# Moving two SBUF tiles by 96 bytes: `region` and `xs` at 448 instead of 32 modulo 512

## The chip, the cores and the metric

The kernel runs on one core of one Trainium2 chip. The metric is the device time of one execution in microseconds (us); the time before is the median of three runs. A profile is a hardware trace of one execution. Its engines are PE (TensorE matmul), PEld (TensorE weight load), DVE (VectorE), ACT (ScalarE), POOL (GpSimd) and SP (SyncE, which issues the DMAs). SBUF is the memory on the chip that the engines read: 128 partitions, and in each of them a tile takes a stretch of bytes. An address below is a byte offset within a partition, given modulo 512.

## The reference, cut to what matters

Two encoder layers over 256 positions of width 1024, in float32. Each layer is half a gated feed-forward block, a mixer, and another half block:

```python
for l in range(DEPTH):
    x = x + 0.5 * swiglu(rmsnorm(x, ffn1_norm[l]), ffn1_w_gu[l], ffn1_w_down[l])
    ...
    x = x + mix
    x = x + 0.5 * swiglu(rmsnorm(x, ffn2_norm[l]), ffn2_w_gu[l], ffn2_w_down[l])
```

`swiglu(h, w_gu, w_down)` splits `h @ w_gu` in two halves of 2816 columns, `g` and `u`, and returns `(silu(g) * u) @ w_down`. The mixer of layer 0 is a chunked spatial gate beside differential attention, that of layer 1 latent attention beside grouped attention with rotary embedding; both have one projection in and one out. The feed-forward products are the bulk of the work.

## The kernel before, in words

**Precision.** A float32 product is made from two parts of each operand. `hi` is the value rounded to the matmul type (`F32R`), `lo` what is left. A product is then hi x hi + lo x hi + hi x lo, three full-rate passes, of which the feed-forward blocks do a part only.

**Weights.** SP's queue loads pieces of 1 MB into four `raw` tiles. For each half of a piece ACT copies it to a `hi` tile and DVE subtracts to get a `lo` tile (`fetch`, line 481); there are six of each. They are used in the order of the program.

**Activations.** `x` stays in SBUF, transposed: model dimension on the partitions, positions along the row. `xs` (line 570) holds its scaled `hi` and `lo` parts, for each of 8 k-tiles 2 x 256 elements, so 2048 bytes a k-tile. `region` is an arena of 11264 elements, which each stage cuts anew: the feed-forward blocks put `hs`, the 22 tiles of hidden activations, in it (2048 bytes each), the mixers their projections and `os_`, the operand of the output product.

**Matmul loops.** A matmul has a stationary operand, which PE loads as weights (128 columns, 512 bytes), and a moving one, which it streams.

- `wide` (line 552), feed-forward: stationary is a 128 x 128 chunk of `hi`, moving is `flat(x2)`, 512 columns, the hi and lo part of one k-tile of `xs` or `hs`; then stationary is the same chunk of `lo`, moving the first 256 of these columns. One such pair for each chunk.
- `dense` (line 544): three matmuls, (xh, wh), (xh, wl), (xl, wh). In `out_product` (line 642) the weights are stationary and 256 columns of `os_` in `region` are moving. In `block` (line 616), the input projections, it is the other way round: stationary are 128 columns of `xs`, and a row of `hi` or `lo` of width `w` is moving: 512 columns mostly, 256 in the odd layer's `k` block and 416 in its `c` block (line 623 has the offset, `k % per * w`).

**The order.** All operations are recorded in a `Program` (line 82), with a cost and a priority each. `schedule` (line 162) lists them by a model of the engines and of free slots, and `emit` (line 274) issues them in that order. What depends on what is found from tile names and the offsets inside a tile (`touched`, line 93); the place of a tile in SBUF plays no part.

**Placement.** `keep(name, ...)` (line 373) makes one tile that lives throughout. Tiles lie one behind another in the order in which they are made, each rounded up to a multiple of 32 bytes, and the first, `t1_0`, starts at 128. `scratch` tiles `t1` (1024 bytes) and `t2` (2048) come first; then 32 small tiles `sm` of 20 elements (96 bytes each with the rounding), which `Turns` hands out in rotation, one after another (line 376); then `gap0`, 128 bytes that nobody uses; `raw`, `hi`, `lo`; `region32`, 21888 bytes; `gx` (with `x`), 8448 bytes; `ident`, `ones`, `onesr`, 512 bytes each; `warm`, one element; `gap1`, unused; `region`, `xs`; and behind them `rr`, `rb`, `acc`, `acc2`, rotary tables and small values.

`warm` (line 450) takes the result of one activation at the start, which makes ACT load a function table early. No operation reads it.

Of the kernel before, what the change touches and what calls it, by code (L numbers as in the profile page):

```python
# [351 lines left out]
def trunk_kernel(ctx: ExitStack, tc: tile.TileContext, a: dict, out: bass.AP):  # L352
# [20 lines left out]
    def keep(nm, *shape, dt=F32):  # L373
        return sb.tile([P, *shape], dt, name=nm)
# [38 lines left out]
    sm = Turns("sm", 32, 20)  # L413
# [33 lines left out]
    nc.vector.memset(ones, 1.0)  # L447
    onesr = keep("onesr", P, dt=F32R)
    nc.vector.tensor_copy(out=onesr, in_=ones)
    warm = keep("warm", 1)  # L450
    nc.scalar.activation(out=warm, in_=ones[:, :1], func=AF.Silu)
    make_identity(nc, ident)
    with lead(90e3):
# [112 lines left out]

    keep("gap1", 32)
    region, xs = keep("region", ARENA, dt=F32R), keep("xs", KT, 2, N, dt=F32R)  # L570
    rr_, rb, acc, acc2 = keep("rr", 2), keep("rb", N), keep("acc", N), keep("acc2", 2, N, dt=F32R)
    rr = [rr_[:, h:h + 1] for h in range(2)]
# [589 lines left out]
```

## Time and profile before

| | |
|---|---|
| time, median of 3 runs | 941.68 us (941.42 to 942.18) |
| the profiled execution | 941.91 us |
| its span, first to last instruction | 940.1 us |
| granted TensorE clock | 0.999 |
| PE busy | 933.7 us, 5564 matmuls |
| DVE busy | 723.9 us |
| ACT busy | 548.3 us |
| DMA, whole span | 167.83 MB, mean 179 GB/s |

The difference between the profiled execution and its span is what lies before the first and behind the last recorded instruction. Matmuls are pipelined: the duration of one runs until its results are out, and the next one starts before that, so the sum of durations is more than the busy time, and the cost of a matmul in a steady loop is the distance from its start to the next start. Nearly every operation has line 285 of the kernel, since `emit` issues it there; groups are told apart by the names of their tiles, `out<-in`, with buffer numbers left out: `bank<-xs,hi` is a matmul into a PSUM bank with `xs` moving and a `hi` tile as weights, or `bank<-hi,xs` the reverse.

### The profile page before, as it was taken

The numbers are of one execution on the slowest core, as the hardware profiler recorded it, in microseconds if no ns is written. First come the engines' busy times: TensorE is split into PE (matmuls) and PEld (weight loads), VectorE is DVE, ScalarE is ACT, GpSimd is POOL, SyncE is SP. The second block draws the span as 40 slices with busy tenths as digits, with TensorE's granted clock in tenths as the row PEclk, the third lists the DMA queues.
The fourth block names the chain that finished last, engine by engine and source line by source line (L and its number), as shares of the span: only waits on it lengthen the run. The fifth ranks groups of instructions, "written<-read, shape, count | busy, mean of one in ns | idle before, by whom it ended". The sixth has DMA issues, their size and how long they took to land.

```text
span 940.1 us, 14528 instructions
## 1 busy us (share of the span) xinstructions
PE 933.7 (99%) x5564; PEld 829.3 (88%) x5564; DVE 723.9 (77%) x1326; ACT 548.3 (58%) x938; POOL 27.5 (3%) x57
## 2 busy tenths in 40 slices
PE   9999999999999999999999999999999999999998
PEld 8888888888899888888888888888989988888887
DVE  7997776579989878876588887756888698878652
ACT  7765655446956656655465666544587566565530
POOL 0910000000000000000000000000000000000000
PEclk9999999999999999999999999999999999999999
DMA  9775555553255555555555555554412355555530
GB/s 337 258 268 180 182 192 204 184 180 135 97 217 174 185 190 204 188 180 186 204 181 192 183 195 205 180 184 163 179 57 86 106 186 201 180 185 201 200 109 22
DMA packets 26421, 167.83 MB, mean 179 GB/s; under 512 B 2928, under 2 KB 5104, under 8 KB 7024
## 3 DMA queue, kind: packets, MB, share of 16 engines
q1 hardware_dynamic: 26352, 166.92, 50.4%
q8 instruction: 43, 0.70, 0.3%
q14 instruction: 26, 0.21, 0.1%
HBM read 165.86 MB, written 1.05 MB: 178 GB/s over the span
## 4 chain that ended last, share of the span: by engine, by line
PE 97%; DVE 1%; ACT 1%; DMA 0%; issue 0%; SPq 0%; ACTq 0%
PE bank L285 97%; DVE t L285 0%; ACT t L285 0%; DMA raw<-in_gu 0%; DVE sm L285 0%; ACT hi L285 0%; DVE region L285 0%; DVE lo L285 0%; ACT L285 0%; DVE hi L285 0%; DVE ssg L285 0%; DVE gx L285 0%; SPq L285 0%; DVE ssc L285 0%; DVE rc L285 0%
## 5 line engine op out<-in xcount | busy, mean ns | idle before, releaser
L285 DVE TENSOR_TENSOR lo<-raw,hi 128x1024 fp32r<-128x1024 f32 (+2 forms) x318 | 382.2, 1203 | 161.6 <-ACT hi L285 155.9
L285 ACT ACTIVATE hi<-raw 128x1024 fp32r<-128x1024 f32 (+3 forms) x310 | 322.7, 1043 | 299.7 <-PE bank L285 188.3
L285 PE MATMUL bank<-xs,hi 128*128 128x512 f32 x1408 | 490.8, 391 | 0.5 <-ACT hi L285 0.5
L285 PE MATMUL bank<-xs,lo 128*128 128x256 f32 x1408 | 398.2, 283 | 0.0
L285 PEld LDWEIGHTS bank<-xs,hi 128*128 128x128 f32 x1408 | 265.4, 188 | 56.2 <-ACT hi L285 0.8
L285 PE MATMUL bank<-region,hi 128*128 128x512 f32 (+1 forms) x982 | 290.8, 357 | 0.0
L285 PEld LDWEIGHTS bank<-xs,lo 128*128 128x128 f32 x1408 | 267.2, 190 | 0.7 <-DVE lo L285 0.7
L285 PE MATMUL bank<-region,lo 128*128 128x256 f32 x832 | 234.2, 282 | 0.0
L285 PEld LDWEIGHTS bank<-region,hi 128*128 128x128 f32 x982 | 173.8, 188 | 27.0
L285 PEld LDWEIGHTS bank<-region,lo 128*128 128x128 f32 x832 | 157.1, 189 | 0.0
L285 ACT ACTIVATE t<-bank 128x256 f32<-128x256 f32 (+1 forms) x201 | 76.8, 401 | 40.5 <-PE bank L285 39.4
L285 PE MATMUL bank<-hi,xs 128*128 128x512 f32 (+2 forms) x256 | 78.5, 381 | 0.0
L285 DVE TENSOR_TENSOR t<-bank,t 128x256 f32<-128x256 f32 x176 | 67.5, 420 | 1.0 <-ACT t L285 1.0
L285 DVE TENSOR_TENSOR t<-t,rb 128x512 f32<-128x512 f32 x88 | 60.3, 688 | 1.2
L285 PEld LDWEIGHTS bank<-hi,xs 128*128 128x128 f32 x256 | 47.1, 188 | 8.5
L285 DVE SCALAR_TENSOR_TENSOR gx<-bank,gx 128x256 f32<-128x256 f32 (+1 forms) x71 | 28.3, 450 | 27.2 <-PE bank L285 27.2
L285 PE MATMUL bank<-lo,xs 128*128 128x512 f32 (+2 forms) x128 | 48.1, 375 | 0.0
L285 DVE TENSOR_TENSOR t<-t,t 128x256 f32<-128x256 f32 (+2 forms) x108 | 45.8, 428 | 0.1
L285 ACT ACTIVATE t<-t 128x256 f32<-128x256 f32 (+2 forms) x98 | 39.1, 406 | 3.1 <-DVE t L285 3.1
L285 DVE TENSOR_TENSOR region<-t,region 128x256 fp32r<-128x256 f32 (+2 forms) x92 | 39.1, 429 | 1.1 <-ACT region L285 1.1
L285 ACT ACTIVATE region<-t 128x256 fp32r<-128x256 f32 (+1 forms) x89 | 35.6, 405 | 1.5 <-DVE t L285 1.2
L285 ACT ACTIVATE xs<-gx 128x256 fp32r<-128x256 f32 x48 | 23.9, 499 | 11.0 <-DVE gx L285 10.2
(128 smaller groups left out, 465.3 us busy)
## 6 DMA issues: line engine op xcount, KB each, us to landing
raw<-in_gu SPq DMA_DIRECT2D x86, 1024.0 KB, 4.8
raw<-in_dn SPq DMA_DIRECT2D x44, 1024.0 KB, 4.8
raw<-in_ev_in SPq DMA_DIRECT2D x10, 1024.0 KB, 4.8
raw<-in_ev_out SPq DMA_DIRECT2D x4, 1024.0 KB, 4.9
raw<-in_od_out SPq DMA_DIRECT2D x4, 1024.0 KB, 4.8
raw<-in_gu SPq DMA_DIRECT2D x8, 256.0 KB, 4.5
raw<-in_od_q SPq DMA_DIRECT2D x2, 1024.0 KB, 4.8
raw<-in_od_c SPq DMA_DIRECT2D x2, 832.0 KB, 4.3
```

The costliest lines, as they stand in the source:

```text
L285: r = fn(*map(real, args), **{k: real(v) for k, v in kw.items()})
```

## The change

`warm` is no tile of its own any more; one of the small rotating tiles takes its place. `gap1` shrinks from 32 to 16 elements (128 to 64 bytes). Both come in front of `region` and `xs`, so these, and all tiles made behind them, start 96 bytes lower: `region` and `xs` at 448 instead of 32 modulo 512. `raw`, `hi`, `lo`, `gx` and the rest in front of them stay where they were.

```diff
@@ -447,7 +447,7 @@
     nc.vector.memset(ones, 1.0)
     onesr = keep("onesr", P, dt=F32R)
     nc.vector.tensor_copy(out=onesr, in_=ones)
-    warm = keep("warm", 1)
+    warm = sm(1)
     nc.scalar.activation(out=warm, in_=ones[:, :1], func=AF.Silu)
     make_identity(nc, ident)
     with lead(90e3):
@@ -566,7 +566,7 @@
-    keep("gap1", 32)
+    keep("gap1", 16)
     region, xs = keep("region", ARENA, dt=F32R), keep("xs", KT, 2, N, dt=F32R)
     rr_, rb, acc, acc2 = keep("rr", 2), keep("rb", N), keep("acc", N), keep("acc2", 2, N, dt=F32R)
     rr = [rr_[:, h:h + 1] for h in range(2)]
```

## The prediction

> **What bounds the kernel now.** I read the page's busy line first, then its chain of work that ended last, then the groups kept apart by shape.
>
> ```profile
> PE 933.7 (99%) x5564; PEld 829.3 (88%) x5564; DVE 723.9 (77%) x1326; ACT 548.3 (58%) x938; POOL 27.5 (3%) x57
> PE 97%; DVE 1%; ACT 1%; DMA 0%; issue 0%; SPq 0%; ACTq 0%
> L285 PE MATMUL bank<-xs,hi 128*128 128x512 f32 x1408 | 490.8, 391 | 0.5 <-ACT hi L285 0.5
> L285 PE MATMUL bank<-xs,lo 128*128 128x256 f32 x1408 | 398.2, 283 | 0.0
> L285 PE MATMUL bank<-region,hi 128*128 128x512 f32 x682 | 236.6, 390 | 0.0
> L285 PE MATMUL bank<-region,lo 128*128 128x256 f32 x832 | 234.2, 282 | 0.0
> L285 PE MATMUL bank<-hi,xs 128*128 128x512 f32 x192 | 63.7, 401 | 0.0
> L285 PE MATMUL bank<-lo,xs 128*128 128x512 f32 x96 | 37.9, 395 | 0.0
> L285 PE MATMUL bank<-region,hi 128*128 128x256 f32 x300 | 54.2, 283 | 0.0
> L451 ACT ACTIVATE warm<-ones x1: 203/203/203, 2.0 to 2.0; 128x1 f32<-128x1 f32 x1
> ```
>
> The reader is to see three things. PE is the chain (97%) and waits for almost nobody: the last column of each group, its idle time, is 0.0 to 0.5 us. Most of it is one pattern, a `hi` matmul of 512 columns followed by a `lo` matmul of 256, from `wide`: 1408 + 682 = 2090 pairs. And a mean duration (391, 283 ns) is longer than the distance between two starts, since matmuls overlap; so the cost of a pair is read from starts, in the timeline of PE.
>
> ```profile
> 300.02 0.39 PE L285 MATMUL bank<-xs,hi 128*128 128x512 f32 x1
> 300.25 0.28 PE L285 MATMUL bank<-xs,lo 128*128 128x256 f32 x1
> 300.37 0.39 PE L285 MATMUL bank<-xs,hi 128*128 128x512 f32 x1
> ...
> 469.54 0.39 PE L285 MATMUL bank<-region,hi 128*128 128x512 f32 x1
> L285 PE MATMUL bank<-xs,hi 128*128 128x512 f32 x314 | 108.9, 390 | 0.0
> L285 PE MATMUL bank<-region,hi 128*128 128x512 f32 x176 | 61.1, 390 | 0.0
> ```
>
> The last two rows count the stretch: 314 + 176 = 490 `hi` matmuls start from 300.02 to 469.54, which are 489 pairs in 169.52 us, **346.7 ns a pair**. 2090 pairs are 724.5 us of the 940.1 us span. Whatever a start address does to this cadence is multiplied by 2090; 1 ns a pair is 2.1 us, or 0.22%.
>
> Is there anything in a pair that an address could take away or add? Here are the other steady loops, by their first and last rows.
>
> ```profile
> 200.57 0.40 PE L285 MATMUL bank<-lo,xs 128*128 128x512 f32 x1
> 211.77 0.40 PE L285 MATMUL bank<-lo,xs 128*128 128x512 f32 x1
> 268.05 0.28 PE L285 MATMUL bank<-region,lo 128*128 128x256 f32 x1
> 268.75 0.28 PE L285 MATMUL bank<-region,lo 128*128 128x256 f32 x1
> 668.59 0.28 PE L285 MATMUL bank<-lo,xs 128*128 128x256 f32 x1
> 670.72 0.28 PE L285 MATMUL bank<-lo,xs 128*128 128x256 f32 x1
> 934.30 0.28 PE L285 MATMUL bank<-region,lo 128*128 128x256 f32 x1
> 936.05 0.28 PE L285 MATMUL bank<-region,lo 128*128 128x256 f32 x1
> 936.36 0.42 DVE L285 SCALAR_TENSOR_TENSOR gx<-bank,gx 128x256 f32<-128x256 f32 x1 [6.82 <-PE bank L285]
> 930.00:935.00 5.00, 5.00 (x46) 1.00 0.08 26
> 269.00:273.00 4.00, 4.00 (x37) 1.00 0.63 252
> ```
>
> `dense` runs in threes, one `lo` to two `hi`. In `block` with 512 columns: 16 threes in 11.20 us, 233.3 ns a matmul. In the output product with 256 columns: two threes in 0.70 us, 116.7 ns. In the `k` block of the odd layer, 256 columns: six threes in 2.13 us, 118.3 ns. At the very end: five threes in 1.75 us, 116.7 ns again. For 768 columns that is 350, 350, 355 and 350 ns, against 346.7 in a pair. The last stretch has DMA at a share of 0.08 and DVE idle for 6.82 us, the stretch around 270 us has DMA at 0.63, and the cadence is the same: neither DMA nor the vector engines set it. What is left is inside PE: its two reads, the streamed operand and the next weights.
>
> One row pair shows that the place of an operand counts at all. In the `c` block a piece holds two k-tiles of 416 columns, 1664 bytes = 3 x 512 + 128, so the streamed weights start at 256 and at 384 modulo 512 in turn, six matmuls each, and nothing else changes.
>
> ```profile
> 673.86 0.54 PE L285 MATMUL bank<-hi,xs 128*128 128x416 f32 x2
> 674.99 0.55 PE L285 MATMUL bank<-hi,xs 128*128 128x416 f32 x2
> 676.14 0.54 PE L285 MATMUL bank<-hi,xs 128*128 128x416 f32 x2
> ```
>
> The first of each row's two matmuls belongs to the group before, so 673.86 to 674.99 holds five matmuls at 256 and one at 384, and 674.99 to 676.14 the reverse: 1.13 and 1.15 us, some 1 to 2%, at the limit of what two digits show.
>
> **The change part by part.** *What moves.* Counting tile sizes from the first tile (128 modulo 512, each tile rounded up to 32 bytes), `raw`, `hi` and `lo` start at 256, `onesr` ends at 384, `warm` takes 32 and `gap1` 128, so `region` and `xs` start at 32. After the change nothing lies between 384 and a gap of 64: 448. The weights stay. Seen from the streamed operand, the weights lay 224 bytes ahead modulo 512; they will lie 320 ahead. In `block`, where `xs` is the weight load, it goes from 288 to 192. Everything behind `xs` (`rr` to `ssg`) moves 96 bytes down too.
>
> *What is added, removed, reordered: nothing.* The order is made from names and offsets inside tiles, which stay. `warm` becomes the first turn of `sm`, so each later small tile takes the next of the 32, and a tile still comes round after 32 calls. The one new tie is that DVE's 33rd small tile writes where ACT wrote at 2.0 us, for 203 ns (the `warm` row); that was over long before. Cost 0; if a wait were issued for it, DVE would stand behind it, some tenths of a us, and DVE has 23% of the span free.
>
> *DVE and ACT on moved tiles.* They read and write `xs`, `region`, `acc`, `rb` at new places. Each is 1% of the chain, so even a few per cent in their operations is worth under 0.5 us either way; I take 0. A faster PE would need `hi` and `lo` sooner, but DVE at 77% and ACT at 58% can give the per cent or two at stake.
>
> *The pair.* No row shows a stream at 448, so I bound it. From below: 512 columns take 0.23 us to the next start, 256 take 0.12 (rows from 300.02), so 256 columns are 0.11 and 768 are 0.33; the remaining 16.7 ns of a pair is the most that could go, 34.9 us. From above: 355 ns, the worst cadence of the loops, +8.3 ns, 17.4 us. Nearest are the loops themselves: the steady ones stand 3.3 ns per 768 columns apart (350 against 346.7), and I use that as the **step**: 2090 x 3.33 ns = 7.0 us. The `block` matmuls (192 + 96 of 512 columns, 67.2 us) and the 450 of the output products and the last tile (52.5 us) can move by the same per cent: about 1.2 us together either way; I take 0.
>
> The sign is the choice. In every full-rate loop above, one of PE's two operands starts 32 bytes off a multiple of 64 (`xs` or `region`) and the other on one (`hi`, `lo`). Afterwards both are on it. If memory is read in aligned pieces of 64 bytes, a 512-column stream touches 32 pieces instead of 33 and a 256-column one 16 instead of 17: it can only lose work. No row shows such pieces; it is an assumption. It gives the sign and not the size, and I take one step.
>
> Sum, against the profiled execution's own 941.91 us (span 940.1 and 1.8 around it): 941.9 - 7.0 = 934.9, and as the median of the three runs is 0.2 lower, **934.7 us**.
>
> **The rivals.**
>
> *No effect, 941.7.* The pair's overhead is PE's own, whatever the addresses. For it: `xs` and `region`, gate-up and down, keep one cadence through 489 pairs, although weights and streams take all relative places in steps of 512 bytes. Against it: 1.13 and 1.15 us in the `c` block. That the change doesn't do what it says (448 not reached, or the modulus not 512) ends here too, and so does a gain in `block` alone, about 1 us. [...]
>
> *Slower: the weight load runs into the stream.* Both reads start together with each matmul. If they collide where their distance modulo 512 is wrong, 224 ahead may be a place that avoids it and 320 one that doesn't: the pair already has the best cadence of all steady loops, and the loops with the load at 288 (`block`, the odd `k`) have 350 and 355. It decides in `wide`, as soon as a pair exceeds 347.6 ns (0.2%). One step is +7.0, 948.7 us; the cadence of the odd `k` block would be 959.1. Against it: the output product has the same 224 and still 350, so the distance isn't what separates these loops.
>
> **How the numbers follow.** Faster 0.46 (one step 0.32; more, down to about 925, 0.14), no effect 0.26, slower 0.28 (up to one step 0.16, beyond it 0.12). The likeliest is one step faster, 934.7. The range from 926 to 949 holds one step of either sign and leaves out some 0.06 below and 0.12 above; the far lower bound (907) needs the whole overhead to go, and I give it almost nothing. Faster and slower hold most of the chance with opposite signs; the forecast's own range is 926 to 940. 0.2%, about 1.9 us, is what a measurement of this kernel can tell from no change: 0.46, 0.26, 0.28.
>
> **What would show it.** The counts of instructions and their order stay; the first `hi` to `hi` distance near 300 us is the test. 343.3 ns: the step is right. 346.7 to the last digit: PE's own overhead. 350 or more: the collision. `block` near 200 us should stay within 3 ns of 233.3; if it moves and the pair doesn't, alignment matters for the weight load and not for the stream. The forecast falls if the cadence stays and the time changes elsewhere, for instance by new idle time of PE behind `hi` or `lo`.

## The result and the profile after

| | before | after |
|---|---|---|
| time, median | 941.74 us | 953.73 us |
| ratio, 95% interval | | 1.0129 [1.0117, 1.0140] |
| profiled execution | 941.91 us | 953.04 us |
| its span | 940.1 us | 951.3 us |
| PE busy | 933.7 us | 944.0 us |

The changed kernel is 1.3% slower, 12 us, where 0.7% faster was forecast. The first view is the changed kernel's page: busy time, chain, and the groups by shape.

```profile
PE 944.0 (99%) x5564; PEld 825.6 (87%) x5564; DVE 726.0 (76%) x1326; ACT 548.9 (58%) x938; POOL 28.2 (3%) x57
PE 96%; DVE 1%; DMA 1%; ACT 1%; SPq 0%; issue 0%; DVEq 0%; ACTq 0%
...
L285 PE MATMUL bank<-xs,hi 128*128 128x512 f32 x1408 | 498.3, 398 | 0.4 <-ACT hi L285 0.4
L285 PE MATMUL bank<-xs,lo 128*128 128x256 f32 x1408 | 396.1, 281 | 0.9 <-DVE lo L285 0.8
L285 PE MATMUL bank<-region,hi 128*128 128x512 f32 x682 | 241.2, 397 | 0.0
```

PE is still the chain and still waits for almost nobody (0.4 and 0.9 us of idle time in the whole span, in the last column); the counts of instructions are the same on every engine. But a `hi` matmul of 512 columns takes 397 to 398 ns where it took 390 to 391, and the `lo` matmul behind it 281 where it took 283. These durations are no costs, but they point at the pair, and at its first half. The timeline of PE near the same place, and the count of `hi` matmuls from 300.1 to 472.6 us:

```profile
299.83 0.40 PE L285 MATMUL bank<-xs,hi 128*128 128x512 f32 x1
300.07 0.28 PE L285 MATMUL bank<-xs,lo 128*128 128x256 f32 x1
300.19 0.40 PE L285 MATMUL bank<-xs,hi 128*128 128x512 f32 x1
...
472.26 0.40 PE L285 MATMUL bank<-region,hi 128*128 128x512 f32 x1
L285 PE MATMUL bank<-xs,hi 128*128 128x512 f32 x319 | 112.8, 397 | 0.0
L285 PE MATMUL bank<-region,hi 128*128 128x512 f32 x170 | 60.1, 397 | 0.0
```

319 + 170 = 489 `hi` matmuls start from 299.83 to 472.26: 488 pairs in 172.43 us, **353.3 ns a pair** against 346.7. Two other loops went the other way. The rows are `block` with 512 columns and the output product.

```profile
201.81 0.39 PE L285 MATMUL bank<-lo,xs 128*128 128x512 f32 x1
212.79 0.39 PE L285 MATMUL bank<-lo,xs 128*128 128x512 f32 x1
276.25 0.28 PE L285 MATMUL bank<-region,lo 128*128 128x256 f32 x1
285.79 0.28 PE L285 MATMUL bank<-region,lo 128*128 128x256 f32 x1
```

16 threes in 10.98 us are 228.8 ns a matmul (233.3 before), 28 threes in 9.54 us are 113.6 ns (116.7 before). Summed over all starts of the two traces, the distances from `hi` to `lo` grew by 13.6 us in the 2090 pairs, those from `lo` to `hi` fell by 0.4, the products with weights stationary and 256 columns fell by 1.0 and the 512-column blocks by 1.0: +11.2 us, which is the difference of the two spans.

### The profile page after: what moved, and what is told of

It is laid out like the page before. It is cut to its first block, busy times and chain, and to the rows that moved or that the text cites. A ratio compares the mean times of both kernels' runs of the same rounds, so it can differ in the third digit from the quotient of the medians.

```text
span 951.3 us, 14528 instructions
## 1 busy us (share of the span) xinstructions
PE 944.0 (99%) x5564; PEld 825.6 (87%) x5564; DVE 726.0 (76%) x1326; ACT 548.9 (58%) x938; POOL 28.2 (3%) x57
## 4 chain that ended last, share of the span: by engine, by line
PE 96%; DVE 1%; DMA 1%; ACT 1%; SPq 0%; issue 0%; DVEq 0%; ACTq 0%
PE bank L285 96%; DMA raw<-in_gu 1%; ACT t L285 1%; DVE t L285 0%; SPq L285 0%; DVE sm L285 0%; DVE lo L285 0%; DVE acc L285 0%; DVE region L285 0%; DVE hi L285 0%; ACT L285 0%; ACT hi L285 0%; DVE ssg L285 0%; DVE gx L285 0%; DVE ssc L285 0%
## 5 line engine op out<-in xcount | busy, mean ns | idle before, releaser
L285 PE MATMUL bank<-xs,hi 128*128 128x512 f32 x1408 | 498.3, 398 | 0.4 <-ACT hi L285 0.4
L285 PE MATMUL bank<-region,hi 128*128 128x512 f32 (+1 forms) x982 | 294.4, 362 | 0.0
L285 PEld LDWEIGHTS bank<-xs,lo 128*128 128x128 f32 x1408 | 264.3, 188 | 2.1 <-DVE lo L285 2.1
L285 PE MATMUL bank<-region,lo 128*128 128x256 f32 x832 | 233.2, 280 | 0.0
```

Of the source, the lines that this page charges most:

```text
L285: r = fn(*map(real, args), **{k: real(v) for k, v in kw.items()})
```

## The experiments

Below, *distance* is the address of the weights minus that of `region` and `xs`, modulo 512: 224 before, 320 after. For each run I give the mean distances between starts in the stretch from 300 to 470 us, which holds only pairs, and where it says more, the means of the other two loops without their stalls. The means of the output product also hold the 66 starts of the same form in the last tile of the last feed-forward block (928 to 936 us in the kernel before).

**What of the change does it: the small tile, the stream's place, or the distance?** Four kernels, one thing each.

```diff
 # e1_warm_only: region and xs stay at 32
-    warm = keep("warm", 1)
+    warm = sm(1)
-    keep("gap1", 32)
+    keep("gap1", 40)
 # e2_gap_only: region and xs at 448, warm a tile of its own
-    keep("gap1", 32)
+    keep("gap1", 8)
 # e3_weights_too: weights at 160, region and xs at 448 (and warm = sm(1))
-    keep("gap0", 32)
+    keep("gap0", 8)
-    keep("gap1", 32)
+    keep("gap1", 40)
 # e4_weights_alone: weights at 352, region and xs at 32 (and warm = sm(1))
-    keep("gap0", 32)
+    keep("gap0", 56)
-    keep("gap1", 32)
+    keep("gap1", 16)
```

> warm becomes a small rotating tile, and the gap grows to 160 bytes, so region and xs stay at 32 modulo 512. Theory (the distance from the streamed operand to the weights, modulo 512, sets the cadence of a pair): 224 as before, hi to lo start 228 ns, 346.7 ns a pair, 941.7 us within 1 us. Rival (the small tile taken out of the rotation matters): some of the 12 us shows here, above 944 us.

> warm stays a tile of its own, the gap is 32 bytes, so region and xs lie at 448 as in the changed kernel, and so does all behind them. Theory and every rival that blames the place: 353.3 ns a pair, 953.7 us. Rival (warm): 941.7 us.

> region and xs at 448 as in the changed kernel, but the gap in front of the raw, hi and lo tiles shrinks by 96 bytes too, so the weights go from 256 to 160 and the distance is 224 again. Distance theory: 346.7 ns a pair, 941.7 us. Rival (the absolute place of the stream, 448, or of what lies behind it): 353.3 ns, 953.7 us.

> region and xs at 32 as before, the weights moved up by 96 bytes to 352, so the distance is 320 as in the changed kernel without moving the stream. Distance theory: 353.3 ns a pair, 953.7 us, and the output product and the 512-column blocks some 2 per cent faster as in the changed kernel. Rival (absolute place of the stream): 346.7 ns, 941.7 us.

| run | weights, stream | distance | pair | time | ratio, interval |
|---|---|---|---|---|---|
| e1_warm_only | 256, 32 | 224 | 346.7 ns | 941.61 us | 0.9999 [0.9990, 1.0009] |
| e2_gap_only | 256, 448 | 320 | 353.3 ns | 953.35 us | 1.0121 [1.0106, 1.0136] |
| e3_weights_too | 160, 448 | 224 | 346.7 ns | 941.61 us | 0.9996 [0.9987, 1.0006] |
| e4_weights_alone | 352, 32 | 320 | 353.3 ns | 953.28 us | 1.0122 [1.0107, 1.0137] |

A quick way to read a cadence is to count PE's matmuls in a fixed stretch. The view is the busy time by windows of PE alone, 300 to 440 us, first of e3_weights_too, then of e4_weights_alone; (x...) is the count.

```profile
300.00:440.00 140.00, 140.00 (x809) 1.00 0.54 188
```

```profile
300.00:440.00 140.00, 140.00 (x794) 1.00 0.53 183
```

The same 140 us, PE busy all the time in both, and 15 matmuls fewer. The stream at 448 is as good as at 32 if the weights follow (e3), and the weights alone cost the whole 12 us without the stream moving (e4). So, as far as two places of each show it, neither place matters in itself; **the distance between them does**. The small tile plays no part. In e4 the output product (114.8 ns) and the blocks (229.4) were faster as well, as in the changed kernel.

**Which distances are dear?** Gaps in front of the weights and of `region` were set for other distances, within the 288 bytes that are free. For 208 and 240, `region` and `xs` were made one tile `rx` whose first 4 elements (16 bytes) are unused, with the order of instructions kept:

```diff
 # d240 (and warm = sm(1)); d208 has gap0 24 and gap1 40
-    region, xs = keep("region", ARENA, dt=F32R), keep("xs", KT, 2, N, dt=F32R)
+    rx = keep("rx", 4 + ARENA + KT * 2 * N, dt=F32R)
+    prog.shift[rx.name] = 4
+    region = rx[:, 4:4 + ARENA]
+    xs = rx[:, 4 + ARENA:].rearrange("p (k z n) -> p k z n", k=KT, z=2)
...
-            off = np.array([ap.offset % pitch])
+            off = np.array([ap.offset % pitch - self.shift.get(name, 0)])
```

> weights at 256, region and xs at 480: distance 288, 32 more than a multiple of 64, as 224 is. Rival A (a distance that is a multiple of 64 is the dear one): 346.7 ns a pair, 941.7 us. Rival B (a certain stretch of distances modulo 512 is dear, with 320 in it, and the cost changes gradually or in steps): from 346.7 to 353.3 ns, between 941 and 954 us.

> weights at 256, region and xs at 0: distance 256, a multiple of 64. Rival A (multiples of 64 are dear): 353.3 ns a pair, 953.7 us. Rival B (a stretch of distances that holds 320 but not 224): nearer to 346.7 ns, 941 to 950 us.

> weights at 224, region and xs at 32: distance 192, a multiple of 64 on the other side of 224. Rival A: 353.3 ns a pair, 953.7 us. Rival B: 346.7 ns or less, 935 to 942 us, if less distance is cheaper all the way.

> weights at 256, region and xs at 416: distance 352, 32 more than a multiple of 64. Rival A: 346.7 ns a pair, 941.7 us. Rival B: 353.3 ns or more, 953 us or more.

> weights at 128, region and xs at 32: distance 96. Theory (the cost of a pair has a period of 128 bytes of distance: 224 and 352, both 96 modulo 128, cost 346.7 ns, 192 and 320, both 64 modulo 128, cost 353): 346.7 ns a pair, 941.7 us within 2. Rival (period 512, 224 and 352 alike by chance): anything from 346 to 356 ns.

> weights at 192, region and xs at 32: distance 160, 32 modulo 128 as 288 is. Theory (period 128): 353.2 ns a pair, 955 us within 2. Rival (period 512): anything from 346 to 356 ns.

> region and xs are one tile whose first 4 elements are left unused, so that they start at 16 modulo 512: distance 240, between 224 (346.7 ns a pair) and 256 (348.5 ns). If the cost changes in steps of 32 bytes or more: one of the two, 941 to 945 us. [...] If there is a better place in between: below 346 ns, under 940 us.

> the same with the weights at 224 and region and xs at 16: distance 208, between 192 (353.2 ns a pair) and 224 (346.7 ns). Steps of 32 bytes or more: one of the two, 941.7 or 955 us. A gradual cost: about 350 ns, 948 us. A better place in between: below 346 ns, under 940 us.

The table gives the means of these runs; "(one)" marks a time from a single execution.

| distance | modulo 128 | hi to lo, ns | lo to hi, ns | pair, ns | output product, ns | block 512, ns | time, us |
|---|---|---|---|---|---|---|---|
| 96 | 96 | 229.3 | 117.3 | 346.7 | 118.2 | 233.4 | 942.5 (one) |
| 160 | 32 | 232.0 | 118.0 | 350.0 | 119.9 | 234.2 | 950.3 (one) |
| 192 | 64 | 234.0 | 119.3 | 353.3 | 117.7 | 233.2 | 956.3 |
| 208 | 80 | 232.7 | 117.3 | 350.0 | 118.3 | 233.2 | 949.9 (one) |
| 224 (before) | 96 | 228.3 | 118.3 | 346.7 | 116.7 | 233.1 | 941.7 |
| 240 | 112 | 225.2 | 121.5 | 346.7 | 115.7 | 231.3 | 940.5 (one) |
| 256 | 0 | 230.1 | 116.5 | 346.7 | 119.8 | 228.3 | 944.0 |
| 288 | 32 | 234.6 | 118.8 | 353.3 | 118.4 | 233.2 | 955.4 |
| 320 (after) | 64 | 235.0 | 118.3 | 353.3 | 114.5 | 229.2 | 953.7 |
| 352 | 96 | 229.2 | 117.5 | 346.7 | 118.5 | 233.4 | 942.2 |

For the four distances with more than one execution the ratios to the kernel before are 1.0141 [1.0112, 1.0170] at 192, 1.0016 [1.0001, 1.0031] at 256, 1.0131 [1.0102, 1.0161] at 288 and 1.0001 [0.9990, 1.0012] at 352.

The same count shows the steps. The windows are of PE from 300 to 440 us, of d96, d208, d192 and d288 in this order:

```profile
300.00:440.00 140.00, 140.00 (x810) 1.00 0.54 188
```

```profile
300.00:440.00 140.00, 140.00 (x802) 1.00 0.54 188
```

```profile
300.00:440.00 140.00, 140.00 (x795) 1.00 0.54 188
```

```profile
300.00:440.00 140.00, 140.00 (x795) 1.00 0.53 186
```

810, 802 and 795 matmuls: nearly equal steps, and d192 and d288 on the same one although their distances from `hi` to `lo` differ by 0.6 ns.

Rival A, that multiples of 64 are dear, falls with 288 (dear, no multiple) and 256 (cheap in this stretch, a multiple; its first block is dear, as the last section shows). Rival B, one dear stretch that holds 320 but not 224, falls with 192: both sides of 224 are dear. A period of 128 bytes was the next theory: 96, 224 and 352 agree, and so do 192 and 320. But 160 and 288 should have agreed and stand at 350.0 and 353.3, so it is no more than a rough rule. What is clear is that the **mean** pair of this stretch is 346.7, 350.0 or 353.3 ns, 3.3 ns apart, at ten distances, and never below 346.7.

The single pairs do not keep to these three values. Four starts of d288 show it; the distance from `hi` to `lo` is 0.24 us, then 0.23:

```profile
299.71 0.40 PE L285 MATMUL bank<-xs,hi 128*128 128x512 f32 x1
299.95 0.28 PE L285 MATMUL bank<-xs,lo 128*128 128x256 f32 x1
300.07 0.39 PE L285 MATMUL bank<-xs,hi 128*128 128x512 f32 x1
300.30 0.28 PE L285 MATMUL bank<-xs,lo 128*128 128x256 f32 x1
```

The trace holds starts in whole ns. In the kernel before every pair of the stretch is 346 or 347 ns, in the changed one 353 or 354. But in d288 pairs of some 346 and 361 ns alternate, in d208 some 346.5 and 353.5, in d160 349 and 351, and d192 goes in threes of about 348, 357 and 354. So the mean of 208 is no cost in between: pairs as at 224 and pairs as at 320 take turns. Why the means come out in equal steps, no run here shows.

**Whose weights?** Within a pair the `lo` weights are loaded during the 512-column stream and the `hi` weights during the 256-column one (in the kernel before, loads of 0.19 us from 300.02 and 300.25 us, where matmuls of 512 and 256 columns start). Only one of the two weight tiles was moved to distance 320:

```diff
 # lo_only: hi at 256, lo at 352, region and xs at 32 (and warm = sm(1))
-    raws_, his, los = Turns("raw", RAW, SUB), Turns("hi", RING, PIECE, F32R), Turns("lo", RING, PIECE, F32R)
+    raws_, his = Turns("raw", RAW, SUB), Turns("hi", RING, PIECE, F32R)
+    keep("gap2", 24)
+    los = Turns("lo", RING, PIECE, F32R)
...
-    keep("gap1", 32)
+    keep("gap1", 16)
 # hi_only: the same with hi and lo exchanged
```

> only the lo weights move, to 352 (320 from the stream); hi stays at 256 (224), region and xs at 32. In a pair, the lo weights are loaded while the 512-column stream of the hi matmul runs. Theory (a stream collides with the load of the weights for the next matmul): the hi to lo distance rises to 235 ns as in the changed kernel, lo to hi stays 118, 353.3 ns a pair, some 954 us. Rival (it is a matmul's own weights): hi to lo stays 228 ns.

> only the hi weights move, to 352 (320); lo stays at 256 (224), region and xs at 32. Theory (load of the next weights): the hi weights are loaded while the 256-column stream runs, where the changed kernel lost nothing; hi to lo stays 228 ns, lo to hi 118, 346.7 ns a pair, 941 to 943 us. Rival (own weights): hi to lo 235 ns, some 954 us.

My theory failed both times. lo_only: 228.3 ns from `hi` to `lo`, 346.7 a pair, 942.42 us, ratio 1.0002 [0.9992, 1.0012]. hi_only: 233.0 and 351.1 ns, 952.12 us, ratio 1.0105 [1.0083, 1.0127]. Windows of PE, lo_only first, then hi_only:

```profile
300.00:440.00 140.00, 140.00 (x810) 1.00 0.54 188
```

```profile
300.00:440.00 140.00, 140.00 (x800) 1.00 0.53 186
```

**In the mean it is the place of the `hi` weights.** They account for 4.4 of the 6.7 ns alone; the rest comes only when both move. The place of the `lo` weights is not without effect, though: in lo_only pairs of some 344 and 349 ns alternate, and only their mean is that of before. hi_only goes in threes of some 357, 354 and 342 ns, and its mean, 351.1, is none of the three values of the table. The timeline of weight loads of the kernel before shows in what the two differ (the matmul starts beside them, 300.02 `hi`, 300.25 `lo`, 300.37 `hi`, are in the prediction):

```profile
300.02 0.19 PEld L285 LDWEIGHTS bank<-xs,lo 128*128 128x128 f32 x1
300.25 0.19 PEld L285 LDWEIGHTS bank<-xs,hi 128*128 128x128 f32 x1
```

Each load starts with the matmul before its own and takes 0.19 us. The `lo` load ends at 300.21, before its matmul starts at 300.25. The `hi` load ends at 300.44, after its matmul started at 300.37. By these rows the `lo` load has 40 ns to spare and the `hi` load has none, so a delay of the one could be hidden and a delay of the other could not. That fits the means of both runs, but it is an argument and not shown. It was not tested by itself, for instance with a longer second stream; no delay is seen in the loads either, since a `hi` load of `wide` is recorded with 188 ns on average before and after. That the two reads collide at all is inferred from the cadence. Whether the `hi` load collides with the 256 columns before its matmul or with the first of its own 512 stays open, since both streams read the same tile.

**A better place for each loop?** In the table the output product is cheapest at 320 and the pair is not. So in os_apart the tiles stand as in d240, and only `os_`, the operand of the output products, is moved inside `region` to distance 320, in both layers:

```diff
         ar, af = Arena(region), Arena(region32)
+        ar(108)
         os_ = ar(2, KT, 2, P)
+        ar(20)
...
-            g = 1 if pitch <= 64 else 16
+            g = 1 if pitch <= 64 else 4 if name in self.shift else 16
```

> distance 240 for xs, the feed-forward operand and the other tiles as in the run with 240, but the output products' operand os_ starts 432 bytes further into region, at distance 320, the one at which the output product was fastest (114.6 ns a matmul against 115.8 at 240 and 116.8 at 224). Theory (each loop pays for its own distance): output product near 114.6 ns, pairs at 346.8 ns, 940.0 us, about 0.2 per cent under the kernel before. Rival (the whole kernel has one best place): no gain over 940.5.

The output product took 113.9 ns a matmul against 115.7 in d240, the pairs 346.7 and the blocks 231.9 (231.3 in d240). So the move changed the loop whose operand moved and left the pair alone. But the whole gain is in the odd layer, 118.3 to 113.8 ns; from 275 to 286 us, in the even layer, the output product takes 113.3 ns in both kernels. At distance 240 the same loop thus ran at 113.3 in one layer and at 118.3 in the other: the distance does not decide alone. The time is 940.35 us (median of 11), against 941.89 for the kernel before; but the ratio, 1.0005 [0.9984, 1.0025], says nothing, because three of the eleven executions lie near 947 and the others from 939.7 to 942.0. So no version here is shown to beat the kernel before.

## Why the prediction was wrong

**What bounds the kernel: right.** PE is the chain and waits for almost nobody, the pair is 346.7 ns 2090 times, and whatever a start address does is multiplied by that. The time went into the pair, as the `hi` to `hi` distance near 300 us, which the prediction had named as the test, showed: 353.3 ns.

**That the place of an operand counts at all: right,** though it was read from 1.13 and 1.15 us, at the edge of two digits. The runs show it plainly: with the same order of matmuls and no idle time of PE from 300 to 470 us, the weights' address alone (e4) takes the pair from 346.7 to 353.3 ns and costs 1.2%.

**The sign: wrong, and this is the step that failed.** "If memory is read in aligned pieces of 64 bytes, a 512-column stream touches 32 pieces instead of 33 and a 256-column one 16 instead of 17: it can only lose work." I called it an assumption, no run shows such pieces, and it gave the sign all the same. The runs show the distance of the two operands in place of the alignment of one: the stream at 448 neither gains nor loses when the weights follow (e3), and at 32 the kernel loses 12 us when the weights move away (e4). Nor does it help that both are aligned: in the changed kernel both start on multiples of 64 and the pair has 353.3 ns; in d256, where both do too, it has 353.3 in the first block and 346.7 in the third, and never less than before. "It can only lose work" looked at each read as if it were alone. What the two reads do to each other stays open.

**The size of a step: right, by luck; their number wrong.** One step was 3.3 ns a pair, 7.0 us, taken from the difference between two loops. The mean pairs of the runs do stand in steps of that size, but no run ties them to that difference: single pairs take other values, and the output product goes from 113.3 to 120.0 ns without such steps. The change took two steps upward: 2090 x 6.67 = 13.9 us, less 2.0 in the other loops (the starts above give 13.2 for the pairs).

**The other loops at nothing: nearly.** They moved together by 2.0 us where some 1.2 were allowed, and against the pair.

**The rival that won** was the third, "the weight load runs into the stream", with its place (`wide`), its mark (over 347.6 ns) and its evidence: the pair already had the best cadence of all steady loops. That none of ten distances gave a mean pair under 346.7 speaks for this evidence. The runs bear out that the distance counts; that it works by a collision is not shown. Its price was one step, 948.7, with 959.1 as the far end; 953.7 lies between. My argument against it, that the output product had 224 as well and still 350 ns for 768 columns, did not hold: the output product changes with the distance too, in another way (means of 113.9 to 119.9 ns).

**The range** ended at 949, so that it held a single step upward and cut off the 355 ns of the worst loop, although that was the named bound. Two steps would have had to be in it.

**What costs nothing did cost nothing:** `warm` in the rotation (e1: 0.9999), DVE and ACT on moved tiles, the tiles behind `xs` (e3 has them at the changed kernel's place: 0.9996).

## What to carry to other kernels

Where PE streams back to back and waits for nobody, as here, the cost of a matmul is the distance between starts, not its duration (in the kernel before a `hi` matmul of a pair lasts 391 ns, and the next matmul starts 228.3 ns after it); compute it over hundreds of matmuls before and after, since the mean duration on the page also moves (391 to 398 ns here) but is no cost, and then look at single pairs, since a mean can hide two that alternate (346 and 361 ns in d288). When a tile moves in SBUF, ask how far it comes to lie from whatever PE reads beside it; in e3 that counted, and the place itself did not (346.7 ns with the stream at 448). If the present placement already has the best cadence of all loops, a move made without a measured reason may have little to gain: of the nine other distances here none gave a faster mean pair and five a slower one throughout.

## What was not expected of the hardware

- The mean cadence of a pair is 346.7, 350.0 or 353.3 ns at ten distances and holds to 0.2 ns from one stretch of 20 us to the next between 300 and 470 us, even where single pairs alternate between values up to 15 ns apart.
- The same loop at the same distance can run at two of them in one execution, so something beside the distance decides too; what it is stays open. d256, windows of PE in the first and the third feed-forward block:

```profile
50.00:190.00 140.00, 140.00 (x794) 1.00 0.56 201
300.00:440.00 140.00, 140.00 (x809) 1.00 0.54 191
```

  794 and 809 matmuls in 140 us are the counts of the changed kernel and of the one before. Its eight times spread from 942.05 to 946.02 us. Whether the three times near 947 of os_apart come from the same was not traced; its profiled execution took 940.16.
- Loops of one kernel can want different distances: by the mean, 320 is the best of ten for the output product and among the worst for the pair. It is a mean over places: at 320 the last tile took 117.8 ns a matmul, and the even layer's output product from 275 to 286 us took 113.3, as at 240.
